# One product for the outputs and the state step of a delta-rule chunk, in a fused convolution and RWKV-7 block

## The chip, the cores and the metric

One core of a Trainium2 chip runs the whole block. The metric is device time in microseconds from launch to end, as the median of several executions. Engines are called PE (TensorE: matmuls, with their weight loads as PEld), DVE (VectorE), ACT (ScalarE), POOL (GpSimd) and SP (SyncE, which issues the DMAs).

## The reference, cut to what matters

The input x is 2048 tokens of 1024 channels, float32, one layer. An RMS norm with an adaptive scale and shift feeds one large input projection. Its parts go to a convolution branch (width 31, per channel) and to an RWKV-7 branch with 16 heads of 64 channels. Both are gated, projected, merged, projected once more and added to x, and a last RMS norm follows. The change lies in the RWKV-7 branch, whose core is a recurrence over tokens on a 64x64 state per head:

```
def step(state, inp):
    r_t, w_t, k_t, v_t, kk_t, b_t = inp
    sk = jnp.einsum('bhvk,bhk->bhv', state, kk_t)
    state = (state * w_t[:, :, None, :] - sk[..., None] * b_t[:, :, None, :]
             + v_t[..., None] * k_t[:, :, None, :])
    return state, jnp.einsum('bhvk,bhk->bhv', state, r_t)
...
o = _rwkv7_scan(r, decay.reshape(hd), k, v, kk, kk * a)
o = _layernorm(o, gn_g.reshape(RWKV_HEADS, RWKV_HEAD), gn_b.reshape(RWKV_HEADS, RWKV_HEAD), GN_EPS)
```

## The kernel before, in words

**Blocks, groups, pairs, chunks.** The 2048 tokens are four blocks of 512 (b). In a block the 1024 RWKV channels are four groups of 256 (g): 16 groups in all. A group is two pairs (q), a pair is two heads (hh) of 64 channels, which fill the 128 partitions. The 512 tokens of a block are eight chunks of 64 (c); chunks are counted in pairs, cc, with e = 0 for the even and 1 for the odd one.

**What fills PE.** For each block, every column tile of the input projection is a product of 24 matmuls (8 tiles of K, each three times, because the operands are split into a high and a low fp32r part) into one of two PSUM banks, ps_main. The order of the projections is written out by hand in FILL and LAST: k, r and v of a pair, then convolution values and gates. The output products of the end of the kernel (`wino`, tiles w_c) go into ps_main as well.

**How the rest is put between.** All other work is written as Python generators, called tasks. While the kernel is built, a planner keeps a modelled clock (`note`, lines 116 to 183, prices each instruction) and lets a task go on when the model says that what it waits for is there. After each matmul of a projection the planner is polled and may put a task's instructions next in the queues of the engines. So the order of every engine's instructions is fixed at build time; on the chip each engine takes its own queue in order and waits for semaphores. In the model an f32 product of PE costs `max(N_, 64) / 600 * 1.04` us if it uses all 128 rows and more than 64 columns of the array, with N_ the moving columns (line 137), about half of that or less if it uses 64 rows or 64 columns (`part`), and a change between the two kinds costs 0.13 or 0.27 us more (line 141).

**A pair** (`pair`, lines 980 to 1117) works on decays and keys and builds, per chunk, two operands in SBUF: KR (decayed kk and r side by side) and BK (scaled kk·a and k side by side). Lines 1071 to 1085 multiply BK by KR for all chunks and both heads, mask the 128x128 results and store them in As: for each pair, head and chunk a 128x128 matrix. Half of its columns belong to r (`rcol`), the other half to kk (`kcol`). These products wait with `joining` (line 298): while a chain runs they are held back by up to JOIN = 6 us unless the last product on PE was of the partial kind. Lines 1087 to 1094 transpose BK on PE into tk, with the two halves of tk's partitions for k and kk·a. At line 1101 the pair waits until the norm of the group two before is through, because uv has two buffers. Pairs run one after the other, and the evacuation of the next pair's k, r and v projections waits for a pair's end (line 1635). BK has one buffer.

**A group** (`group`, lines 1131 to 1362) sends the kk blocks of As through DRAM into a layout where POOL inverts 64 triangular 32x32 blocks at once (lines 1146 to 1175, tiles La, TT, itmp), gets them back into As, and in a locked stretch (lines 1211 to 1270, in which no other task may take a PSUM bank of the small pools) completes the inverses of the 64x64 triangles (Tn) and multiplies tk and the r columns of As by them (py, pg). From there on tk holds, per chunk, the k rows and the inverse-multiplied kk rows; As holds the matching r columns.

**The chain** (lines 1275 to 1314) is the loop over the eight chunks, in which the state S of the group's four heads is carried along. For each chunk c:

- PE: KR times S, two products (q) into columns 0 and 1 of the PSUM bank xo of that parity (`b_`); half of the partitions are the outputs' part from the old state, the other half what is needed for uv.
- ACT: Se = S times the chunk's decay pe, two instructions. DVE: adds the PSUM half to uv, 64x256.
- PE: state increment tk times uv, in an even chunk as two 128x128 products with 128 moving columns, in an odd chunk as four products of 64 columns by head.
- DVE: S = increment times pe plus Se, four instructions of 64x64.
- Only after an odd chunk: PE adds the r columns of As times uv for both chunks of the pair, eight products of 64 array columns and 64 moving columns, and ACT copies both output halves into O (which is uv's memory).

**The norm** (lines 1317 to 1362) normalizes O per head. For each of the two pairs in turn it waits until the gate projection exists (`G.gated`), loads two tiles zb and zr, transposes four 128x128 pieces of O into the bank late, scales on ACT, adds and multiplies on POOL and stores to z_d. `G.normed` is set at the second pair.

Of the kernel before, what the change touches and what calls it, by code (L numbers as in the profile page):

```python
# [82 lines left out]
def hybrid_block(ctx: ExitStack, tc: tile.TileContext, x, vecs, convk, w2a2, final_g, ada, w_in, w_co, w_ro, w_o, crow, out,  # L83
# [896 lines left out]
    def pair(G, q_, box):  # L980
# [105 lines left out]

        tk = l3.tile([P, NCH, P], F32, name="tk", tag="tk", bufs=TKB)
# [31 lines left out]
    def opened(b, g, h, lora):  # L1119
        G = Group()  # L1120
        G.b, G.g, G.h, G.lora, G.tri, G.pairs, G.chained, G.gated, G.normed = b, g, h, lora, 0, 0, False, False, False
        G.merged = False
# [8 lines left out]
    def group(G, before):  # L1131
# [18 lines left out]
        for half in range(2):  # L1150
            nc.sync.dma_start(La[64 * half:64 * half + 64], dAl)
        TT = lt.tile([P, 16, 32], F32, name="TT", tag="TT", bufs=1)
# [25 lines left out]
        for half in range(2):  # L1178
            nc.sync.dma_start(dTl[half], TT[64 * half:64 * half + 64])
        yield ok(dT)  # L1180
# [54 lines left out]

        def banks():
            return [p_.tile([P, NCH // 2, P], F32, name=n_, tag=n_) for p_, n_ in ((pl, "late"), (pa, "aux"))]
# [11 lines left out]
        with tc.high_priority(HP):  # L1249
# [23 lines left out]
        yield step(*tk)  # L1273
# [3 lines left out]
        for c in range(NCH):  # L1277
# [975 lines left out]
```

## Time and profile before

| | us |
|---|---|
| median of 3 runs | 2713.66 |
| lowest, highest | 2713.03, 2714.61 |
| the profiled execution, its own time | 2703.53 |
| its span, first to last instruction | 2701.8 |

The profile is one execution, and its durations belong to that one. Its time is 10.1 us below the median of the runs. Granted TensorE clock over the span: 0.989.

How to read it: nearly all instructions carry line 194, because a helper records every operation for the planner; so groups are told apart by their tiles, written out<-in with buffer numbers left out. "128*128" behind a PE instruction are the rows and columns of the array that it uses, the two sizes behind it are what moves through and how much, "x4" is how many instructions a row gathers. In a group's row, the numbers behind the bar are the busy time in us, the mean duration of one in ns, and the idle time of the engine just before them with what ended it.

| tiles | what it is |
|---|---|
| ps_main | projections and output products |
| aux<-KR,BK | the products of `pair` that become As |
| aux<-ident,BK | transposes into tk |
| xo<-S,KR | chain: old state |
| xo<-uv,tk | chain: state increment |
| xo<-uv,As, 128*64 | chain: outputs (64*64 is the locked stretch) |
| late<-ident,uv | transposes of the norm |

### The profile page before, as it was taken

The page shows a single profiled execution, that of the slowest core. Times are in us where ns is not written, and L with a number is a line of the kernel's source. Part 1 is how long each engine was busy: PE and PEld are TensorE (multiplying, and loading weights), DVE is VectorE, ACT ScalarE, POOL GpSimd, SP SyncE. Part 2 cuts the span into 40 slices and gives each one's busy share as a digit, 9 for nine tenths or more (in the row PEclk, how much of TensorE's full clock was granted, in tenths as well). Part 3 has the DMA queues.
Part 4 walks back from the last instruction along what each step waited for, and adds up shares of the span by engine and source line. Part 5 has one row for each costly group of instructions (what it writes and reads, how often), then busy time and mean ns, then how long its engine had stood idle before and what let it go on. Part 6 is the DMA issues. An engine that isn't in the chain of part 4 may idle for free.

```text
span 2701.8 us, 51029 instructions
## 1 busy us (share of the span) xinstructions
PE 2598.4 (96%) x18417; PEld 2092.2 (77%) x18417; DVE 2217.9 (82%) x3808; ACT 1188.2 (44%) x2343; POOL 1309.1 (48%) x1807
## 2 busy tenths in 40 slices
PE   6999999999999999999999999999999987899997
PEld 5778787887887887788888778788788766688886
DVE  7787889888879897888887878888988699888586
ACT  5544444453443433453434333434343454456443
POOL 1575748461738374626482857583716486000000
PEclk9999999999999999999999999999999998999999
DMA  9887778786877788868786888687756778789874
GB/s 346 277 297 268 270 255 282 264 277 221 275 237 266 224 290 268 267 202 274 231 281 214 293 282 262 236 285 231 241 170 219 251 251 285 252 319 333 313 265 164
DMA packets 396142, 705.04 MB, mean 261 GB/s; under 512 B 137065, under 2 KB 153777, under 8 KB 395889
## 3 DMA queue, kind: packets, MB, share of 16 engines
q1 hardware_dynamic: 395888, 701.78, 77.1%
q8 instruction: 145, 2.38, 0.4%
q14 instruction: 109, 0.88, 0.1%
HBM read 487.26 MB, written 213.26 MB: 259 GB/s over the span
## 4 chain that ended last, share of the span: by engine, by line
PE 51%; DVE 4%; DMA 2%; issue 1%; POOL 1%; ACT 0%; SPq 0%; DVEq 0%; ACTq 0%; POOLq 0%
PE ps_main L194 43%; PE aux L194 4%; PE xo L194 3%; PE late L194 2%; POOL w_c L194 1%; DVE S L194 0%; DVE cells L194 0%; DVE fc L194 0%; DVE h_lo L194 0%; DMA w_lo<-kl_in 0%; DMA hf<-xT 0%; DVE mr L194 0%; DVE As L194 0%; SPq L194 0%; DMA dn<-dN 0%
## 5 line engine op out<-in xcount | busy, mean ns | idle before, releaser
L194 PE MATMUL ps_main<-h_hi,w_hi 128*128 128x512 f32 x2304 | 925.8, 402 | 10.6 <-DVE lora L194 4.7
L194 PE MATMUL ps_main<-h_hi,w_lo 128*128 128x512 f32 x2304 | 922.0, 400 | 4.7 <-POOL w_lo L194 2.7
L194 PE MATMUL ps_main<-h_lo,w_hi 128*128 128x512 f32 x2304 | 923.3, 401 | 0.0
L194 DVE SCALAR_TENSOR_TENSOR acc<-u,ck,acc 128x512 f32<-128x512 f32 x928 | 698.2, 752 | 25.4 <-DVE acc L194 0.5
L194 PEld LDWEIGHTS ps_main<-h_hi,w_hi 128*128 128x128 f32 x2304 | 434.5, 189 | 108.5 <-issue 8.9
L194 PEld LDWEIGHTS ps_main<-h_hi,w_lo 128*128 128x128 f32 x2304 | 434.5, 189 | 101.5 <-POOL w_lo L194 4.9
L194 PEld LDWEIGHTS ps_main<-h_lo,w_hi 128*128 128x128 f32 x2304 | 434.6, 189 | 93.6 <-issue 5.7
L194 PE MATMUL ps_main<-h_hi,w_c 128*128 128x512 f32 x896 | 294.5, 406 | 19.3 <-DVE mr L194 9.4
L194 ACT ACTIVATE th<-ps_main 128x512 f32<-128x512 f32 x160 | 95.9, 599 | 348.6 <-PE ps_main L194 302.1
L194 POOL TENSOR_TENSOR TT<-TT,itmp 128x126 f32<-128x126 f32 (+22 forms) x496 | 211.8, 427 | 38.9
L194 POOL TENSOR_TENSOR itmp<-La,TT 128x126 f32<-128x126 f32 (+22 forms) x496 | 207.5, 418 | 41.5 <-issue 8.2
L194 PEld LDWEIGHTS ps_main<-h_hi,w_c 128*128 128x128 f32 x896 | 172.9, 193 | 63.5 <-issue 9.1
L194 POOL TENSOR_TENSOR w_lo<-w_st,w_hi 128x1024 fp32r<-128x1024 f32 x53 | 128.8, 2431 | 153.4 <-ACT w_hi L194 141.0
L194 PE MATMUL ps_main<-h_lo,w_c 128*128 128x512 f32 x448 | 182.1, 406 | 12.3 <-DVE h_lo L194 12.3
L194 ACT COPY uv<-xo 64x256 f32<-64x256 f32 (+1 forms) x192 | 81.1, 439 | 250.1 <-PE xo L194 188.5
L194 DVE SCALAR_TENSOR_TENSOR S<-xo,pe,Se 64x64 f32<-64x64 f32 x512 | 123.0, 280 | 51.0 <-PE xo L194 38.0
L194 PE MATMUL ps_main<-w_c,h_hi 128*128 128x512 f32 x448 | 140.0, 393 | 0.0
L194 ACT CAST w_c<-w_raw 128x512 fp32r<-128x512 f32 x168 | 102.8, 618 | 83.9 <-DMA w_raw<-wk_o 32.9
L194 DVE TENSOR_TENSOR As<-aux,maskA 128x512 f32<-128x512 f32 x128 | 82.4, 685 | 57.2 <-PE aux L194 56.6
L194 PEld LDWEIGHTS ps_main<-h_lo,w_c 128*128 128x128 f32 x448 | 86.5, 193 | 34.5 <-DVE h_lo L194 15.7
L194 ACT ACTIVATE t<-ps_main,mu 128x512 f32<-128x512 f32 x96 | 66.0, 687 | 107.2 <-PE ps_main L194 100.9
L194 ACT ACTIVATE Se<-S,pe 128x128 f32<-128x128 f32 x256 | 88.7, 395 | 43.5 <-DVE S L194 42.7
(294 smaller groups left out, 4559.2 us busy)
## 6 DMA issues: line engine op xcount, KB each, us to landing
w_hi<-kh_in SPq DMA_DIRECT2D x219, 512.0 KB
w_lo<-kl_in SPq DMA_DIRECT2D x219, 512.0 KB
w_st<-w_in_t SPq DMA_DIRECT2D x73, 512.0 KB
kh_in<-w_hi SPq DMA_DIRECT2D x71, 512.0 KB
kl_in<-w_lo SPq DMA_DIRECT2D x71, 512.0 KB
lny<-y_d SPq DMA_DIRECT2D x80, 256.0 KB
w_raw<-wk_o SPq DMA_DIRECT2D x56, 256.0 KB
ada_st<-ada_t SPq DMA_DIRECT2D x16, 512.0 KB
```

Source lines behind the costliest of these rows:

```text
L194: r = f(*a, **k)
```

## The change

As and tk are put side by side in one 128x128 matrix. After the locked stretch, its r columns are as before, and its kk columns, which are no longer needed, are overwritten with the values of tk: the k rows by four copies on ACT, the inverse-multiplied kk rows by the four copies on DVE that went to tk before. One product of As with uv then gives a chunk's outputs on one half of the partitions and the state increment on the other. It is done in each chunk, even or odd, in four products (pair and head) with all 128 columns of the array and 64 moving columns, added onto the outputs' part that KR times S left in the bank; the other half of the bank, whose value was added to uv, is set to zero by a memset first. The decay that the four DVE instructions multiplied in is now taken into BK before the transposes, by eight ACT instructions of 128x128 for each pair, after the products of BK and KR have read it. The state step becomes two DVE adds of 64x128. ACT copies the outputs after each chunk, 64x256 at a time, as many copies as before.

Two more edits: a group clears TT only when the group before has sent off its inverses (`inverted`); and the norm transposes and scales both pairs first, sets `normed`, and only then waits for the gate and loads zb and zr for each pair.

```diff
@@ pair, between the products for As and the transposes into tk
+        for c4 in range(NCH // 4):
+            yield used_up(BK)
+            for c in range(c4 * 4, c4 * 4 + 4):
+                bk = BK[:, c // 2, c % 2 * 128:c % 2 * 128 + 128]
+                nc.scalar.mul(bk, bk, pe[:, c:c + 1])
...
@@ group, before TT is cleared
+        yield when(lambda: before is None or before.inverted)
         TT = lt.tile([P, 16, 32], F32, name="TT", tag="TT", bufs=1)
...
@@ group, locked stretch
             for e in range(2):
                 for q in range(2):
-                    nc.vector.tensor_copy(tk[q][prow(e), e::2, :], py[q][prow(e)])
-        yield both(step(*tk), bank("late"))
+                    nc.scalar.copy(As[q][vrow(e), :, e::2, kcol(e)], by_head(tk[q][vrow(e), e::2, :]))
+            for e in range(2):
+                for q in range(2):
+                    nc.vector.tensor_copy(As[q][prow(e), :, e::2, kcol(e)], by_head(py[q][prow(e)]))
+        yield both(step(*As), bank("late"))
...
@@ group, chain
                 nc.vector.tensor_tensor(out=uv[pr_, c], in0=b_[pr_, 0:2], in1=uv[pr_, c], op=ALU.add)
-            yield step(uv)
-            if e == 0:
-                for q in range(2):
-                    nc.tensor.matmul(b_[:, 2 + q, :], R[q]["tk"][:, c, :], uv[:, c, q, :], start=False, stop=(q == 1),
-                                     skip_group_check=True)
-            else:
-                for q, hh, hs in every:
-                    nc.tensor.matmul(b_[hs, 2 + q, 0:64], R[q]["tk"][:, c, hs], uv[:, c, q, hs], start=False,
-                                     stop=(q + hh == 2), skip_group_check=True)
-            if e:
-                for n, (q, hh, hs) in enumerate(every):
-                    for i in range(2):
-                        nc.tensor.matmul(xo[i][vrow(i), q, hs], As[q][:, hh, c - 1 + i, rcol(i)], uv[:, c - 1 + i, q, hs],
-                                         start=False, stop=(n == 3), skip_group_check=True)
+                nc.vector.memset(b_[pr_, 0:2], 0.0)
+            yield step(uv, b_)
+            for n, (q, hh, hs) in enumerate(every):
+                nc.tensor.matmul(b_[:, q, hs], As[q][:, hh, c, :], uv[:, c, q, hs], start=False, stop=(n == 3),
+                                 skip_group_check=True)
             with tc.high_priority(HP):
-                for q, hh, hs in every:
-                    nc.vector.scalar_tensor_tensor(out=Sg[hs, q, hs], in0=b_[hs, 2 + q, slice(0, 64) if e else hs],
-                                                   scalar=R[q]["pe"][hs, c:c + 1], in1=Se[hs, q, hs],
-                                                   op0=ALU.mult, op1=ALU.add)
-            if e:
-                with tc.high_priority(HP):
-                    for i in range(2):
-                        nc.scalar.copy(O[vrow(i), cc], xo[i][vrow(i), 0:2])
+                for hs in (slice(0, 64), slice(64, 128)):
+                    nc.vector.tensor_tensor(out=Sg[hs, :, hs], in0=b_[pr_, 0:2, hs], in1=Se[hs, :, hs], op=ALU.add)
+                nc.scalar.copy(O[vrow(e), cc], b_[vrow(e), 0:2])
...
@@ group, norm
-        yield when(lambda: G.gated)
+        ocs = []
         for q in range(2):
...
+            ocs.append(oc)
+        G.normed = True
+        for q, oc in enumerate(ocs):
+            pr = 2 * g + q
+            yield both(when(lambda: G.gated), hx.room(2))
+            zb, zr = hx.take("zb"), hx.take("zr")
+            nc.sync.dma_start(zb, bv_dram[b][pr])
+            nc.sync.dma_start(zr, ro_dram[b][pr])
```

More of the change, by code (lines that the diff above doesn't have):

```diff
@@ L1121, in opened @@
         G.b, G.g, G.h, G.lora, G.tri, G.pairs, G.chained, G.gated, G.normed = b, g, h, lora, 0, 0, False, False, False
-        G.merged = False
+        G.merged = G.inverted = False
         G.prior, G.uv, G.As = Gs[-2] if len(Gs) > 1 else None, None, []
@@ L1179, in group @@
             nc.sync.dma_start(dTl[half], TT[64 * half:64 * half + 64])
+        G.inverted = True
         yield ok(dT)
@@ L1234, in group, with by_head @@
         yield both(step(Tn, uv), bank("xo", 2))
+        def by_head(t_):
+            return t_.rearrange("p c (h n) -> p h c n", h=2)
         def banks():
@@ L1272, in group @@
         Sg = S[g]
-        yield step(*tk)
+        yield step(*As)
         xo = [px.tile([P, 4, P], F32, name="xo", tag="xo") for _ in range(2)]
@@ L1342, in group @@
         yield ok(uv)
-        yield when(lambda: G.gated)
+        ocs = []
         for q in range(2):
             pr = 2 * g + q
-            yield hx.room(2)
-            zb, zr = hx.take("zb"), hx.take("zr")
-            nc.sync.dma_start(zb, bv_dram[b][pr])
-            nc.sync.dma_start(zr, ro_dram[b][pr])
             yield burst(free, bank("late"))
```

1 line of the change is left out of this document (removed).

## The prediction

> **What bounds the kernel now.** I read the busy table first, then the chain of waits, then the busy time by stages, then the groups of instructions by shape, and last the timeline around single products.
>
> ```profile
> PE 2598.4 (96%) x18417; PEld 2092.2 (77%) x18417; DVE 2217.9 (82%) x3808; ACT 1188.2 (44%) x2343; POOL 1309.1 (48%) x1807
> ...
> PE 51%; DVE 4%; DMA 2%; issue 1%; POOL 1%; ACT 0%; SPq 0%; DVEq 0%; ACTq 0%; POOLq 0%
> ```
>
> ```profile
> 50.00:2147.00 2097.00, 2063.19 (x15711) 1664.32 (x15710) 1734.84 (x2958) 891.92 (x1783) 1199.20 (x1724) 1.00 0.77 255
> 2147.00:2390.00 243.00, 208.16 (x1275) 161.10 (x1274) 214.16 (x337) 113.38 (x211) 108.54 (x74) 0.94 0.78 265
> ```
>
> The columns of the second fence are the stretch, its length, and the busy time of PE, weight loads, DVE, ACT and POOL. From 50 to 2147 us, where the sixteen groups run, PE is busy 2063 of 2097 us at full clock (the 1.00 behind POOL); only 34 us are idle. No other engine there is above 83% (DVE 1735 of 2097). So a microsecond added to PE's queue in this stage is a microsecond of time, and a microsecond saved elsewhere is worth at most a part of those 34. From 2147 to 2390 it is different: PE has 35 us of idle time, and DVE is 88% busy.
>
> What the chain's own products cost on PE is not their busy time, because matmuls overlap. It is what they push apart in the row of ps_main products.
>
> ```profile
> 253.17 0.39 PE L194 MATMUL ps_main<-h_hi,w_hi 128*128 128x512 f32 x1
> 253.40 0.39 PE L194 MATMUL ps_main<-h_lo,w_hi 128*128 128x512 f32 x1
> 253.63 0.60 PE L194 MATMUL xo<-S,KR 128*128 128x128 f32 x4
> ...
> 254.30 0.40 PE L194 MATMUL ps_main<-h_hi,w_hi 128*128 128x512 f32 x1
> ```
>
> ```profile
> 260.59 0.39 PE L194 MATMUL ps_main<-h_lo,w_hi 128*128 128x512 f32 x1
> 260.82 0.60 PE L194 MATMUL xo<-uv,tk 128*128 128x128 f32 x4
> ...
> 261.50 0.39 PE L194 MATMUL ps_main<-h_hi,w_hi 128*128 128x512 f32 x1
> ```
>
> ```profile
> 1338.11 0.40 PE L194 MATMUL ps_main<-h_lo,w_hi 128*128 128x512 f32 x1
> 1338.44 0.46 PE L194 MATMUL xo<-uv,tk 128*64 128x64 f32 x8
> 1338.72 0.64 PE L194 MATMUL xo<-uv,As 128*64 128x64 f32 x16
> ...
> 1339.63 0.40 PE L194 MATMUL ps_main<-h_hi,w_hi 128*128 128x512 f32 x1
> ```
>
> Undisturbed ps_main products stand 0.23 us apart (253.17 to 253.40). I measure from the last ps_main start ahead of a burst to the second one behind it, since the first behind it comes early and the second late, and take off two steps, 0.46. The KR·S burst then costs 254.30 − 253.40 − 0.46 = 0.44, the increment of an even chunk 261.50 − 260.59 − 0.46 = 0.45, and the increment of an odd chunk with the outputs of both chunks 1339.63 − 1338.11 − 0.46 = 1.06 us. Each f32 product is two instructions, so those bursts are 2, 2 and 4 + 8 products.
>
> **The change: PE.** There are 16 groups of 4 chunk pairs, 64 pairs. KR·S stays. Removed per pair: 0.45 + 1.06 = 1.51 us. Added per pair: two bursts of four products, weights 128x128 (As), only 64 columns moving, so 8 instructions each. The trace has no such shape. What sets its pace is the weight load.
>
> ```profile
> L194 PEld LDWEIGHTS xo<-S,KR 128*128 128x128 f32 x512 | 74.8, 190 | 17.0 <-issue 6.8 <-DVE S L194 0.6
> ...
> L194 PEld LDWEIGHTS xo<-uv,As 128*64 128x64 f32 x1024 | 35.8, 138 | 0.0
> ```
>
> ```profile
> 257.27 0.19 PEld L194 LDWEIGHTS ps_main<-h_lo,w_hi 128*128 128x128 f32 x1
> 257.37 0.19 PEld L194 LDWEIGHTS ps_main<-h_hi,w_lo 128*128 128x128 f32 x1
> ```
>
> A load of 64 columns lasts 138 ns and one of 128 columns 190: 0.8 ns per column on top of a fixed part. At 257.27 two full loads follow each other with no product between (behind a burst of another shape) and stand 0.10 us apart: that is the pace of loads alone. The KR·S burst, four loads and four products of 128 columns in 0.44 to 0.45, has a pace of 0.112. With 64 columns moving the product gets shorter but its load does not, so I price an instruction at 0.112 again: 8 × 0.112 = 0.90 us per chunk. Bounds: the pace of 64-column work from the odd burst, 8 instructions from 1338.44 to 1338.72, alternating between two column halves, so 0.07 each and 0.56 in all; and above, load and half-length product one after the other, 0.11 + 0.05, 1.28 in all. I take 0.90 because the nearest row, KR·S, has the same weights and shows the load fully overlapped. Per pair 1.80 − 1.51 = +0.29, times 64: **+18.4 us**. The bounds give −25 and +67.
>
> [...]
>
> **The change: lost company.** The odd burst works on 64-column halves of the array, KR·BK of the next pair on 64-row halves; call both tiled. The planner likes to put them side by side (line 303 holds KR·BK back by up to 6 us for it while a chain runs).
>
> ```profile
> 255.00 0.39 PE L194 MATMUL ps_main<-h_hi,w_hi 128*128 128x512 f32 x1
> ...
> 255.60 0.64 PE L194 MATMUL xo<-uv,As 128*64 128x64 f32 x16
> 256.18 1.16 PE L194 MATMUL aux<-KR,BK 64*128 64x128 f32 x16
> ...
> 257.61 0.40 PE L194 MATMUL ps_main<-h_hi,w_lo 128*128 128x512 f32 x1
> ```
>
> ```profile
> 136.50 0.39 PE L194 MATMUL ps_main<-h_hi,w_lo 128*128 128x512 f32 x1
> 136.82 1.16 PE L194 MATMUL aux<-KR,BK 64*128 64x128 f32 x16
> ...
> 138.26 0.40 PE L194 MATMUL ps_main<-h_lo,w_hi 128*128 128x512 f32 x1
> ```
>
> ```profile
> 2007.96 0.64 PE L194 MATMUL xo<-uv,As 128*64 128x64 f32 x16
> 2008.54 1.16 PE L194 MATMUL aux<-KR,BK 64*128 64x128 f32 x16
> ```
>
> Together they cost 257.61 − 255.00 − 0.46 = 2.15; alone 1.06 and 1.30: 0.21 saved each time. It happens 18 times in the timeline, first at 256.18, last at 2008.54. With no tiled burst left in the chain there is nothing to join: 18 × 0.21 = **+3.8 us** (0 if as many find another partner).
>
> **The change: DVE, ACT, POOL, SP.**
>
> ```profile
> L194 DVE SCALAR_TENSOR_TENSOR S<-xo,pe,Se 64x64 f32<-64x64 f32 x512 | 123.0, 280 | 51.0 <-PE xo L194 38.0 <-issue 4.7 <-ACT tk L194 2.4
> ...
> L194 DVE TENSOR_TENSOR uv<-xo,uv 64x256 f32<-64x256 f32 x128 | 53.9, 421 | 29.0 <-PE xo L194 25.2 <-ACT Se L194 1.0
> ...
> L194 DVE MEMSET S<- 128x256 f32 x4 | 1.1, 272 | 0.1
> ```
>
> ```profile
> L194 ACT ACTIVATE Se<-S,pe 128x128 f32<-128x128 f32 x256 | 88.7, 395 | 43.5 <-DVE S L194 42.7
> ...
> L194 ACT COPY uv<-xo 64x512 f32<-64x512 f32 x64 | 34.1, 582 | 100.7 <-PE xo L194 100.5
> ```
>
> DVE per chunk: four increments go, 123.0 / 128 = 0.96 us. A memset of 64x256 comes, between 0.27 (the SBUF memset as wide) and 0.42 (the add of that shape in PSUM), and two adds of 64x128, 0.29 each by interpolating 280 and 421. Net −0.11 to +0.04, times 128: −14 to +5 us on an engine that does not bound; worth nothing by itself. The copies of the inverse keep their count and size, into As instead of tk.
>
> ACT: 256 decay scalings of 128x128, priced by the Se row, 89 us; 64 copies of 64x512 (tk into As), 34 to 37 us. The output copies stay at 128 of 64x256. ACT in the group stage goes from 892 to about 1016 of 2097 us: free time hides it, 49% busy. Queued behind four scalings (1.4 us) are evacuations of ps_main; PE has two banks and a projection is 24 × 0.23 = 5.5 us, so that stays covered.
>
> The pair task gets a new wait: the scalings start only when both KR·BK bursts have read BK, and the transposes into tk wait for all eight, 2.8 us, part of it beside the mask products that free the aux banks anyway. I take +2 us per pair. Who waits: the next pair's k evacuation.
>
> ```profile
> 108.53 1.31 POOL L194 TENSOR_TENSOR vv<-rk,vv 128x512 f32<-128x512 f32 x1
> ```
>
> ```profile
> 110.63 0.74 DVE L194 SCALAR_TENSOR_TENSOR k<-ps_main,v,t 128x511 f32<-128x511 f32 x1
> ```
>
> ```profile
> 274.22 1.28 POOL L194 TENSOR_TENSOR vv<-rk,vv 128x512 f32<-128x512 f32 x1 [6.68 <-ACT Se L194]
> ```
>
> ```profile
> 298.07 0.72 DVE L194 SCALAR_TENSOR_TENSOR k<-ps_main,v,t 128x511 f32<-128x511 f32 x1
> ```
>
> The first pair ends at 109.84 and the next k follows at 110.63: no cover, so +2 once. The fourth ends at 275.50, 22.6 us ahead; such a cover hides it. Without it the cost would be 32 × 2 = 64 us. Sum of this: **+2** (0 to 4).
>
> In the locked stretch ACT copies tk into As behind the four uv copies, 4 × 0.58, so the chain starts about 2 us later; PE has projections meanwhile: nothing. The wait for the prior inversion before TT's memset is met long before in all groups but perhaps the last: nothing, 4 us at most. Norm: two transposes move ahead of two loads each on SP; uv is released earlier, and the group results are needed only after 2147: −1, between −6 and +6, since the stage from 2147 is bound by DVE and moving work between POOL and DVE there can go either way.
>
> **Idle time of the chain.**
>
> ```profile
> L194 PE MATMUL xo<-S,KR 128*128 128x128 f32 x512 | 79.7, 278 | 4.7 <-DVE S L194 4.5
> ...
> L194 PE MATMUL xo<-uv,tk 128*128 128x128 f32 x256 | 42.1, 289 | 10.2 <-DVE uv L194 9.1
> ```
>
> PE lost 14.9 us here to a late DVE. The planner (line 137) prices the new product by its 64 columns, 4 × 0.11 = 0.44, where I expect 0.90, so PE will arrive later than planned and find DVE ready more often. I give back a third, **−5 us** (−15 if all goes, +10 if the new order brings as much as it has brought here).
>
> **Sum**: 18.4 + 3.8 + 2 − 1 − 5 = +18.2 us. The profiled execution took 2703.53 us (span 2701.8 and 1.7 around it), 10.1 below the median of the runs, 2713.66. So 2721.7 in such an execution, and 2713.66 + 18.2 = **2731.9** as a median. By the bounds of the smaller terms (0 to 3.8, 0 to 4, −6 to +6, −15 to +10) this forecast's own range is 2718 to 2748.
>
> **Rivals.** *The product is paced by its 64 moving columns.* For it: the 0.07 of 64-column work, and one array shape for the whole chain. Against: loads in a row 0.10 apart with no product between. Price: 8 × 0.07 = 0.56, so 1.12 − 1.51 = −0.39 per pair, −25, and with the other terms −25.2: 2688. It decides if the new burst stands below 0.75. Chance 0.08. [...]
>
> *No change.* The product costs what I say, but nearly all idle time of the chain goes (−15) and the last stage gains (−6): 18.4 + 3.8 + 2 − 15 − 6 = +3.2: 2717. For it: the idle time is there. Against: much of it is a few single long waits that any order can have. Chance 0.12.
>
> *Pairs become late.* ACT, fuller, takes 10 us more per pair in place of 2 and covers of 10 to 20 us begin to fail in about one pair of three, 2 us each: +22 more: 2754. Against: the cover of 22.6. Chance 0.06.
>
> *Load and short product don't overlap:* 1.28 per chunk, +67 in place of 18.4: 2780. Against: the KR·S burst. Chance 0.04.
>
> **Numbers.** Forecast 0.70, rivals 0.08, 0.12, 0.06, 0.04. 0.2% is 5.4 us, about what a measurement of this kernel can tell from no change. Slower by more: 0.70 + 0.06 + 0.04 = 0.80; within: 0.12; faster: 0.08. The range 2712 to 2748 holds the forecast and the no-change case and leaves out 0.18.
>
> **What the profile after would show.** Right: bursts xo<-uv,As 128*128 128x64 x8 that cost 0.90 by the same measure, loads 0.11 apart; no KR·BK behind a tiled burst, all 64 at 1.30; the group stage longer by 15 to 25 us with PE still at 98%; ACT near 1314 us; DVE nearly as before; a longer wait at 110 us. Wrong: bursts of 0.6 or less; or PE's idle time in the group stage moved by more than 15 us; or many pairs whose next k evacuation waits for them.

## The result and the profile after

The kernel after takes **2758.4 us** at the median (2753.8 to 2761.7), the kernel before 2714.1 beside it: a ratio of **1.0169, 95% interval 1.0153 to 1.0184**, 44 us slower. The sign was forecast, the size was not: 2731.9 was the number, 2748 the upper end. The profiled execution after took 2759.96 us, 56.4 more than that of before, which lay some 10 us below its own median. The accounts below are made of these two executions, so they have to explain 56, not 44; the 12 between are taken for idle and slow time of single executions, since a kernel's instructions are the same each time; that was not shown. Three single executions of kernels further down took 4297, 5836 and 9328 us; they are left out of medians and ratios.

The busy table after, and the shares of the chain of waits:

```profile
PE 2633.2 (95%) x17649; PEld 2142.8 (78%) x17649; DVE 2177.4 (79%) x3684; ACT 1290.7 (47%) x2663; POOL 1293.7 (47%) x1803
...
PE 80%; DVE 7%; DMA 5%; issue 3%; ACT 2%; POOL 2%; SPq 2%; DVEq 0%; ACTq 0%; POOLq 0%
```

The same by stages, cut where before was cut, 3 us behind the start of the last stage (2143.8 us before, 2193.0 after):

```profile
50.00:2196.00 2146.00, 2094.42 (x15001) 1708.93 (x15000) 1703.85 (x2839) 993.14 (x2095) 1190.16 (x1725) 0.99 0.75 250
2196.00:2439.00 243.00, 206.41 (x1198) 163.39 (x1197) 196.41 (x320) 110.81 (x213) 102.34 (x69) 0.93 0.75 250
```

The group stage is longer by 49 us (2097 to 2146), and that is nearly the whole loss. PE is busy 31 us more in it (2063.2 to 2094.4) and idle 18 us more (33.8 to 51.6); and the granted clock, 1.00 before, is 0.99, so some of the 31 is not work either.

A chunk's new burst in the timeline, with nothing beside it:

```profile
262.71 0.39 PE L194 MATMUL ps_main<-h_lo,w_hi 128*128 128x512 f32 x1
262.94 0.39 PE L194 MATMUL ps_main<-h_hi,w_lo 128*128 128x512 f32 x1
263.17 1.00 PE L194 MATMUL xo<-uv,As 128*128 128x64 f32 x8
263.98 0.48 PE L194 MATMUL ps_main<-h_hi,w_hi 128*128 128x512 f32 x1
264.29 0.40 PE L194 MATMUL ps_main<-h_lo,w_hi 128*128 128x512 f32 x1
```

By the measure of the prediction it costs 264.29 − 262.94 − 0.46 = 0.89 us; the median over all bursts of eight between two ps_main products is 0.895. The price was 0.90. The groups that answer to those of before, busy time and mean of one, then the idle time ahead of them and what ended it:

```profile
L194 PE MATMUL ps_main<-h_hi,w_hi 128*128 128x512 f32 x2304 | 926.8, 402 | 27.1 <-DVE k L194 11.9 <-DVE lora L194 4.7 <-issue 2.3
...
L194 PE MATMUL xo<-uv,As 128*128 128x64 f32 x1024 | 131.6, 272 | 10.0 <-DVE xo L194 9.3
...
L194 ACT ACTIVATE BK<-BK,pe 128x128 f32<-128x128 f32 x256 | 80.7, 391 | 21.2 <-PE aux L194 21.1
...
L194 DVE TENSOR_TENSOR S<-xo,Se 64x128 f32<-64x128 f32 x256 | 73.6, 288 | 56.7 <-PE xo L194 45.0 <-issue 6.8 <-ACT ta L194 1.6
...
L194 ACT COPY As<-tk 64x512 f32<-64x512 f32 x64 | 36.4, 618 | 0.2
...
L194 DVE MEMSET xo<- 64x256 f32 x128 | 34.8, 272 | 15.9
```

The first row is the news. In the kernel before it reads as follows; the wait for k, 1.0 us there, is not among its three longest:

```profile
L194 PE MATMUL ps_main<-h_hi,w_hi 128*128 128x512 f32 x2304 | 925.8, 402 | 10.6 <-DVE lora L194 4.7 <-DVE r L194 1.8 <-DVE vv L194 1.2
```

**An account that closes.** From the starts of all products in a trace I took, for each stretch between two ps_main products, the pace of what lies between: 0.2295 us for a ps_main product, 0.112 for a 128-column one, the measured pace of the smaller shapes (KR·BK alone, sixteen instructions, costs 1.30), 0.215 for each entry into tiled work (joined, KR·BK and the odd burst cost 2.15, alone 1.30 and 1.06). What a stretch takes beyond that is idle time or slow clock. Before: work other than ps_main 460.7 us, idle and slow 63.6 in the group stage and 56.3 in the last. After: 482.0, 94.5 and 60.1. So +21.3 of work, +30.9 and +3.8 of idle and slow time: 56.0 of 56.4. (By the medians the last two come to some 23, an estimate: 44 less the work.) Work was forecast at +22.2. The miss is idle time in the group stage.

**Where it is.** The first pair, in the timeline of the kernel after:

```profile
110.18 1.29 POOL L194 TENSOR_TENSOR vv<-rk,vv 128x512 f32<-128x512 f32 x1 [2.88 <-ACT rk L194]
...
110.86 0.40 PE L194 MATMUL ps_main<-h_hi,w_lo 128*128 128x512 f32 x1
...
111.20 1.04 ACT L194 CAST w_hi<-w_st 128x1024 fp32r<-128x1024 f32 x1
...
112.27 0.69 ACT L194 ACTIVATE t<-ps_main,mu 128x512 f32<-128x512 f32 x1
...
113.59 0.75 DVE L194 SCALAR_TENSOR_TENSOR k<-ps_main,v,t 128x511 f32<-128x511 f32 x1 [0.43 <-ACT carry L194]
...
114.39 0.79 PE L194 MATMUL ps_main<-h_hi,w_hi 128*128 128x512 f32 x1 [3.14 <-DVE k L194]
...
114.99 0.63 PE L194 MATMUL ps_main<-h_lo,w_hi 128*128 128x512 f32 x1
...
119.68 0.63 PE L194 MATMUL aux<-lw,wlo 128*128 128x512 f32 x1
...
120.70 0.39 PE L194 MATMUL ps_main<-h_hi,w_lo 128*128 128x512 f32 x1
120.93 0.40 PE L194 MATMUL ps_main<-h_hi,w_hi 128*128 128x512 f32 x1
```

In the kernel before, ACT's first step for k ran ahead of the pair's end:

```profile
107.13 0.69 ACT L194 ACTIVATE t<-ps_main,mu 128x512 f32<-128x512 f32 x1
```

The pair's last product on GpSimd ends at 111.47 (before: 109.84), and k follows 2.1 us later, where it was 0.8. So k is 3.0 us late, and only 1.6 of it is the pair: the rest is ACT's queue, where t now stands behind the pair's last copies and a cast of weights of 1.04 us. PE waits 3.14 us. Then comes what the forecast had no term for: from 114.39 to past 119.68 products take 0.63 us and come 0.43 apart instead of 0.39 and 0.23, so PE ran at half clock for 6 us and lost some 2.7 more. The granted clock, the third number from the right, says the same, 0.50; below it the kernel with JOIN 0.0, whose first pair makes PE wait 3.15 us:

```profile
110.30:113.60 3.30, 0.96 (x5) 1.00 0.47 179
113.70:120.40 6.70, 6.00 (x14) 0.50 0.90 294
120.60:124.00 3.40, 3.40 (x17) 1.00 0.00 0
```

```profile
114.30:117.50 3.20, 3.20 (x9) 0.50 0.98 293
117.80:121.00 3.20, 3.20 (x15) 1.00 0.37 138
```

So with the same wait came half clock for 6.8 us in one kernel and for 3.4 in another. All such stretches in the traces, but for the one that a trace ends in, last 3.4 us or a multiple of it (3.41, 6.83 and 10.24 in the kernels before and after). In the kernel after the 432nd ps_main product starts 5.7 us later than before; the term for this pair was 2. Half clock also came with a wait of 1.91 us, at 1905.8 in the kernel with the scaling alone, and with one of 2.40 us, at 2222.7 in the kernel after (0.50 from 2223.0 to 2229.8), while one of 2.43 us, at 1882.9 in the kernel after, was not followed by it: the length of a wait alone doesn't tell.

The worst one stands near the end of the groups:

```profile
2091.66 11.83 DVE L194 SCALAR_TENSOR_TENSOR acc<-u,ck,acc 128x512 f32<-128x512 f32 x15
...
2098.54 1.27 POOL L194 TENSOR_TENSOR vv<-rk,vv 128x512 f32<-128x512 f32 x1
...
2103.40 0.74 DVE L194 SCALAR_TENSOR_TENSOR k<-ps_main,v,t 128x511 f32<-128x511 f32 x1
2104.06 0.74 DVE L194 SCALAR_TENSOR_TENSOR r<-ps_main,v,t 128x511 f32<-128x511 f32 x1
...
2104.19 0.79 PE L194 MATMUL ps_main<-h_hi,w_hi 128*128 128x512 f32 x1 [5.98 <-DVE k L194]
2104.78 0.63 PE L194 MATMUL ps_main<-h_lo,w_hi 128*128 128x512 f32 x1
2105.21 0.63 PE L194 MATMUL ps_main<-h_hi,w_lo 128*128 128x512 f32 x1
```

The pair is late (its last product ends at 2099.81), k comes 3.6 us after that, behind the last of the fifteen convolution taps on VectorE, and PE waits 5.98 us and goes on at half clock. ACT had done its part for k by 2100.48, so VectorE's queue makes most of the delay behind the pair. In all PE waits for k 5 times, 11.9 us, where before had 1.0; and undisturbed ps_main products at half clock cost 11.6 us in the group stage against 3.1. That is 19 of the 31. Of the other 12, some 7 are a balance of many waits for others, up or down by a few us each, and the rest isn't resolved. Where idle time lies is not yet what caused it; that is for the experiments.

### The profile page after: what moved, and what is told of

Same layout as the page of the kernel before. It is cut to its first block, busy times and chain, and to the rows that moved or that the text cites. A ratio compares the mean times of both kernels' runs of the same rounds, so it can differ in the third digit from the quotient of the medians.

```text
span 2758.2 us, 49724 instructions
## 1 busy us (share of the span) xinstructions
PE 2633.2 (95%) x17649; PEld 2142.8 (78%) x17649; DVE 2177.4 (79%) x3684; ACT 1290.7 (47%) x2663; POOL 1293.7 (47%) x1803
## 4 chain that ended last, share of the span: by engine, by line
PE 80%; DVE 7%; DMA 5%; issue 3%; ACT 2%; POOL 2%; SPq 2%; DVEq 0%; ACTq 0%; POOLq 0%
PE ps_main L194 64%; PE aux L194 6%; PE xo L194 6%; PE late L194 3%; SPq L194 2%; DMA w_lo<-kl_in 1%; DVE acc L194 1%; PE ps_f L194 1%; DVE h_lo L194 1%; DMA w_st<-w_in_t 1%; DMA hf<-xT 0%; DVE mr L194 0%; DVE w_lo L194 0%; DMA lny<-y_d 0%; DVE As L194 0%
## 5 line engine op out<-in xcount | busy, mean ns | idle before, releaser
L194 PE MATMUL ps_main<-h_hi,w_hi 128*128 128x512 f32 x2304 | 926.8, 402 | 27.1 <-DVE k L194 11.9
L194 POOL TENSOR_TENSOR itmp<-La,TT 128x126 f32<-128x126 f32 (+22 forms) x496 | 206.9, 417 | 41.9 <-issue 11.9
L194 POOL TENSOR_TENSOR TT<-TT,itmp 128x126 f32<-128x126 f32 (+22 forms) x496 | 204.4, 412 | 38.9
L194 PEld LDWEIGHTS xo<-uv,As 128*128 128x128 f32 (+1 forms) x2048 | 164.2, 165 | 30.9 <-DVE xo L194 15.3
L194 PE MATMUL xo<-uv,As 128*128 128x64 f32 (+1 forms) x2048 | 166.5, 247 | 13.0 <-DVE xo L194 9.3
L194 ACT CAST w_c<-w_raw 128x512 fp32r<-128x512 f32 x168 | 102.5, 618 | 73.6 <-DMA w_raw<-wk_o 32.8
L194 DVE TENSOR_TENSOR S<-xo,Se 64x128 f32<-64x128 f32 x256 | 73.6, 288 | 56.7 <-PE xo L194 45.0
```

Of the source, the lines that this page charges most:

```text
L194: r = f(*a, **k)
```

## The experiments

Ratios are to the kernel before, measured on the same chip, with 95% intervals; before took 2711 us at the median in all of them. Differences between kernels are of their medians. The first theory was that late pairs lose the time (scalings and the hold of line 303), with rivals in the planner's price, VectorE's zeroing, and the edits of order.

**Decay back in the state step** (after, BK unscaled):

```
-                nc.scalar.mul(bk, bk, pe[:, c:c + 1])
...
-                    nc.vector.tensor_tensor(out=Sg[hs, :, hs], in0=b_[pr_, 0:2, hs], in1=Se[hs, :, hs], op=ALU.add)
+                    nc.vector.scalar_tensor_tensor(out=Sg[hs, q, hs], in0=b_[pr_, q, hs], scalar=R[q]["pe"][hs, c:c + 1],
+                                                   in1=Se[hs, q, hs], op0=ALU.mult, op1=ALU.add)
```

> The change with one part undone: BK is not scaled, and the decay is multiplied in at the state step again, by four DVE instructions of 64x64 in place of two adds. The chain's new product stays. Late pairs (my theory): the longer pairs and the halved clock after the stalls they make are most of the 26 us that the prediction missed, so this gives back 12 to 22 us of the 44: 2736 to 2746 us, with the waits of ps_main for k (12.7 us in the changed kernel's group stage) below 3. Rival, mispriced product: the order of the queues is wrong because the planner takes 0.44 for 0.90 us, which stays: 2752 to 2762. Rival, the memset in the chain: stays too, and DVE gets 0.4 us more per chunk: 2758 to 2770.

Measured: 2775.2 us, 1.0234 (1.0214 to 1.0253), 17 slower than after. A miss for the theory: PE's waits for k did go (1.0 us), yet the idle and slow time of the group stage was 101.8. The 512 scaled adds came back for 256 plain ones, 123.1 us busy on VectorE for 73.6; that these 50 us are the reason is not shown.

**Only the scaling** (before, with BK scaled and plain adds of 64x64):

> The kernel before with one part of the change alone: BK is scaled by the decay on ACT before the transposes, and the state step adds without multiplying, still in four instructions; the chain's products, the norm and the rest are as before. Late pairs: PE work is unchanged, but pairs end 3 to 5 us later, which stalls the first and the last pairs and drops the clock: 8 to 20 us over before, 2722 to 2734. Both rivals: no change, 2711 to 2717.

Measured: 2712.8 us, 1.0007 (0.9997 to 1.0017): no change in the time, as both rivals said, again a miss for the theory. Yet PE waits for k 3 times, 7.9 us, where before had 1.0: the lateness is there. The adds, 0.218 us against 0.280, free 31 us of VectorE; that this is what pays for it is argued, not shown.

**No hold** (after, JOIN 6.0 to 0.0):

> The changed kernel, with the constant JOIN set from 6 to 0, so that KR and BK products are no longer held back for a tiled partner that the new chain never offers. Late pairs: pairs that meet a chain end up to 12 us earlier, so 5 to 15 us are given back: 2743 to 2753. Mispriced product and memset: no change, 2754 to 2762.

Measured: 2737.3 us, 1.0093 (1.0076 to 1.0109): 21 us, half of the loss, come back, more than any of the theories said. Its ps_main row:

```profile
L194 PE MATMUL ps_main<-h_hi,w_hi 128*128 128x512 f32 x2304 | 928.2, 403 | 20.9 <-DVE k L194 7.5 <-DVE vv L194 5.8 <-DVE lora L194 4.7
```

Idle and slow time of the group stage is 68.8, near the 63.6 of before, at the same work (482.0). So in this kernel holding KR·BK back for a burst that no longer exists costs 21 us. What is left, 26 us over before, is little more than the 21.3 of work.

**The planner's price put right** (after; line 137 prices a full-width product by at least 128 columns):

```
-                c = max(N_, 64) / 600 * (0.27 if M_ <= 64 and K_ <= 64 else 0.53 if part else 1.04)
+                c = max(N_, 64 if part else 128) / 600 * (0.27 if M_ <= 64 and K_ <= 64 else 0.53 if part else 1.04)
```

> The changed kernel, with the planner's price of a full-width product raised to that of 128 columns if fewer move, so 0.22 us for each product of the chain in place of 0.11; nothing else. Mispriced product: idle time of PE in the group stage falls by 12 to 25 us: 2733 to 2746. Late pairs: the pairs stay as long, the planner only knows better when PE comes: 2750 to 2760.

Measured: 2757.2 us, 1.0163 (1.0147 to 1.018), no different from after, as the theory of late pairs said. The wrong price is not the cause.

**No hold, in the kernel before** (JOIN 0.0):

> The kernel before with JOIN 6.0 set to 0.0, so that a chunk's KR.BK pair never waits for a partial-row burst to join. Theory (the hold pays where it has a partner: joined, the pair spares the array its change of mode, and only in the kernel after, where no partial-row burst is left, is it a bare delay): 2715 to 2726 us, 4 to 15 slower, with the KR,BK burst at about 1.5 us alone, as after. Rival (a held pair is a late pair in either kernel, partner or not, and what JOIN 0.0 gave after, 21 us, comes here too): 2690 to 2705 us. Rival (the hold matters only once the pairs have lost their slack to the chain's longer bursts): 2709 to 2715 us.

Measured: 2705.4 us, 0.9984 (0.9971 to 0.9997). Outside all three: slightly faster, 6 us, though half the joined bursts are gone (9 in the trace for 18). The hold is no gain there, and far from 21 us of loss.

**An idle product in each chunk's burst** (before):

```
+    zero = cst.tile([P, 8], F32, name="zero")
...
+            nc.tensor.matmul(b_[:, 2, 64:72], R[0]["tk"][:, c, :], zero, start=False, stop=False, skip_group_check=True)
```

> The kernel before with one idle product more in each chunk's burst: the 128x128 tile of tk again, against 8 columns of zeros, 128 times in all, priced as low by the planner as the new product is after; nothing else moves. By the load pace of the trace (0.224 us for one 128-column f32 product) that is 28.7 us of TensorE work. Theory (TensorE work in the chain's bursts costs the kernel its own time, once, and the rest of what after lost comes from elsewhere): 2736 to 2746 us. Rival (work put into the chain's bursts draws waits and half-clock stretches after it, so that each microsecond costs about two, as 21 of work went with 31 of idle and slow clock after): 2755 to 2775. Rival (idle time of the chain absorbs it): 2711 to 2725.

Measured: 2758.1 us, 1.0176 (1.016 to 1.0193), 47 more, which looked like the rival. It was spoilt: the 32 bytes of zeros at the start of the constants moved every later tile, see the shift below. With JOIN 0.0 beside it:

> The kernel before with JOIN 0.0 and the same idle product in each chunk's burst (28.7 us of TensorE work). Theory (the hold is what made 47 us out of 28.7): 2705 and 28.7, so 2728 to 2739 us. Rival (work in the chain's bursts costs more than itself with or without the hold): 2745 to 2757.

Measured: 2747.9 us, 1.0136 (1.0114 to 1.0158), spoilt in the same way.

**Three products of four** (after; the second head of the second pair is left out):

> The kernel after with the fourth product of each chunk's burst left out (the second head of the second pair: its state increment and its output are then not computed); every other operation is as after. TensorE has 128 x 0.224 = 28.7 us less work, 7 less than before has. Theory (work costs its own time once, the hold and the later pairs the rest): 2725 to 2735 us. Rival (idle and slow clock follow the work): 2700 to 2716. Rival (the loss is held up by VectorE's queue and the late pairs, not by TensorE's work): 2745 to 2758.

Measured: 2752.9 us, 1.0151 (1.0134 to 1.0167), as the last of the three said. The work fell to 453.1 us as meant, and idle and slow time rose to 115.0:

```profile
L194 PE MATMUL ps_main<-h_hi,w_hi 128*128 128x512 f32 x2304 | 929.4, 403 | 37.1 <-DVE k L194 23.7 <-DVE lora L194 4.7 <-DVE vv L194 2.3
```

A shorter burst gained 5 us for 29 of work. PE waited 23.7 us for k, 12 more than after, which is over half of the 20.5 that idle and slow time rose by. That late pairs are the limit here is argued, not shown.

**The edits of order alone** (before, with the wait for the inverse and the norm's two pairs first):

> The kernel before with only the two edits of order: the next group's matrices wait until the group before has its inverted ones, and the norm turns both pairs before it takes up the gate. Every theory that puts the loss into the product, the hold and the pairs says no change: 2707 to 2717 us. Rival (the norm's edits, which let the next group's banks and the gate's buffers go at other times, are where the 31 us of idle come from): 2725 to 2745.

Measured: 2720.5 us, 1.0035 (1.0023 to 1.0048): 9 us slower, between the two. Its idle time lies in the last stage (74.5 against 56.3), where the trace has one wait of 16.35 us, at 2293.5, for the norm's work on GpSimd. To see the same edits in the new kernel I undid them there, with and without the hold.

**The product without the edits of order**, JOIN 0.0 and JOIN 6.0:

> The kernel after with JOIN 6.0 set to 0.0 and the norm's edits and the inverted wait undone: of the change only the product, its zeroing and the decay in tk are left. Theory (three causes that add: 21 us of TensorE work, the hold, the norm's edits): the kernel before with JOIN 0.0 took 2705 us, and 21 of work makes 2727: 2720 to 2732 us. Rival (the work draws waits after it, as the dose on the kernel before did, 47 us for 28.7): 2737 to 2750. Rival (the norm's edits cost nothing here): 2735 to 2740, as with JOIN 0.0 alone.

> The kernel after with only the norm's edits and the inverted wait undone, JOIN 6.0 left. Theory (the three causes add): 9 us less than after, 2744 to 2753 us. Rival (with the hold the pairs are late whatever the norm does): 2755 to 2761. Rival (late pairs and the norm's order feed each other): under 2740.

Measured: 2747.2 us (1.014, 1.012 to 1.0159) and 2774.3 us (1.0237, 1.0215 to 1.0259). Both theories of adding causes fail: here the edits gain 10 to 16 us instead of costing 9. The first run lies in the range of the rival by which work draws waits, the second outside all three. The hold costs 27. The profiled execution with the hold took 2786.5 us, 12 above its median, so its rows are high. Its ps_main row:

```profile
L194 PE MATMUL ps_main<-h_hi,w_hi 128*128 128x512 f32 x2304 | 931.1, 404 | 34.0 <-DVE k L194 16.6 <-ACT h_hi L194 7.1 <-DVE lora L194 4.7
```

and without it:

```profile
L194 PE MATMUL ps_main<-h_hi,w_hi 128*128 128x512 f32 x2304 | 926.9, 402 | 16.3 <-DVE k L194 7.9 <-DVE lora L194 4.7 <-DVE th L194 1.6
```

**Three products of four, JOIN 0.0, old order:**

> As the product with JOIN 0.0 and the old norm, but with the fourth product of each chunk's burst left out (the second head of the second pair is then not computed), 28.7 us less TensorE work. Theory (work counts once): 28.7 less than the whole product there, so 2693 to 2705 us. Rival (the end is set by the last pairs and the last group's inverse on GpSimd, and not by TensorE's work): within 8 us of the whole product, 2715 to 2732.

Measured: 2707.4 us, 0.9995 (0.9984 to 1.0007): 40 less than with four, for 28.7 us of work, which lies between the two ranges. Without the hold, TensorE's work counts, and by the account some 10 us of idle and slow time in the group stage went with it. Against the three of four with hold and new order it is 46 us less.

**The shift alone** (before, with the 8 columns of zeros and nothing that uses them):

> The kernel before with nothing but 32 bytes more per partition at the start of the constants, so that every later tile lies 32 bytes further on; no instruction uses them. In both runs with the idle product, whose zeros lay there, the 128x512 products came 234 ns apart at the median instead of 230, and there are 8928 of them. Theory (the shift of the addresses is what slowed them, and so some 30 of the dose's 47 us): 2736 to 2746 us, with a median step of 233 to 235 ns. Rival (the idle product slowed them): 2707 to 2717 us at 230 ns.

Measured: 2727.8 us, 1.0065 (1.0045 to 1.0086): 17 slower, between the two ranges, though the products do step at 234 ns at the median, as in the two other kernels with the shift; all seventeen without it have 230 or 231. Thirty-three undisturbed steps of the kernel before, first and last:

```profile
1014.11 0.39 PE L194 MATMUL ps_main<-h_hi,w_lo 128*128 128x512 f32 x1
...
1021.66 0.39 PE L194 MATMUL ps_main<-h_hi,w_lo 128*128 128x512 f32 x1
```

and forty-one with the shift:

```profile
1009.68 0.39 PE L194 MATMUL ps_main<-h_hi,w_lo 128*128 128x512 f32 x1
...
1019.25 0.40 PE L194 MATMUL ps_main<-h_lo,w_hi 128*128 128x512 f32 x1
```

7.55 / 33 = 0.2288 us against 9.57 / 41 = 0.2334, with the same products in the same order. The steps of before vary by place: the mean of the some 7800 undisturbed ones went from 229.9 to 233.3 ns, 27 us in sum, where the kernel lost 17. Where the rest came back isn't shown.

**The idle product without the shift** (its zeros in 512 bytes behind the weights and activations):

> The kernel before with the idle product in each chunk's burst again, its zeros now in a tile of 512 bytes behind the weights and activations, so that no operand of the 128x512 products is moved by less than that. In the first dose the even burst grew by 0.227 us and the odd one by 0.118, so the dose is 22 us of TensorE work. Theory (work in the chain's bursts costs its own time, once): 2729 to 2738 us, the products 230 ns apart. Rival (work draws idle time after it): 2745 to 2760.

Measured: 2740.7 us, 1.0117 (1.0099 to 1.0134), 30 more (27 to 36), between theory and rival. An even chunk's burst:

```profile
260.50 0.39 PE L194 MATMUL ps_main<-h_hi,w_hi 128*128 128x512 f32 x1
260.73 0.39 PE L194 MATMUL ps_main<-h_lo,w_hi 128*128 128x512 f32 x1
260.96 0.33 PE L194 MATMUL xo<-zero,tk 128*128 128x64 f32 x2
261.13 0.66 PE L194 MATMUL xo<-uv,tk 128*128 128x128 f32 x4
261.55 0.48 PE L194 MATMUL ps_main<-h_hi,w_lo 128*128 128x512 f32 x1
261.87 0.40 PE L194 MATMUL ps_main<-h_hi,w_hi 128*128 128x512 f32 x1
```

It costs 261.87 − 260.73 − 0.46 = 0.68, at the median 0.227 more than before; the odd burst grew by 0.166. That makes 64 × 0.227 + 64 × 0.166 = 25 us of work (28 by the account) for 27 to 36 us of time: work in the chain's bursts costs itself, or a little more, and its idle and slow time in the group stage is near that of before (64.9).

**A blind hold** (before, line 303 without `and not kind[0]`, so that a partner no longer ends the wait):

> The kernel before with the hold made blind: while a chain is open, a KR.BK pair always waits its 6 us, and a partial-row burst no longer ends the wait. No work is added or taken. Theory (the hold without a partner is what makes the idle and half-clock time of after: 26 us there, 57 with the old norm): 2731 to 2765 us, and the idle and slow time of the group stage 25 to 55 us above that of before. Rival (the hold costs only beside the longer bursts of the new product): 2707 to 2720.

Measured: 2704.8 us, 0.9975 (0.9965 to 0.9985): the theory fails, the kernel gains 6 us, though only 1 joined burst is left of 18. With JOIN 0.0 (2705.4) it is the fastest that computes all, ahead of both given ones. A hold that never waits and one that always does gain the same here, so a difference of 6 us between two planned orders says little about the part that was changed.

**The blind hold with the idle product, and with the scaling:**

> The kernel before with the blind hold and the idle product of the clean dose together. Alone the blind hold took 6 us off (2705) and the dose put 30 on (2741). Theory (the hold costs where the chain's bursts are longer on TensorE): 20 to 50 us over the sum of the two, 2755 to 2785 us. Rival (the two only add; the length of the bursts is not what makes the hold dear): 2729 to 2742.

> The kernel before with the blind hold and the scaling of BK by the decay together (the state step as plain adds). Alone the scaling changed nothing (1.0007) and the blind hold took 6 us off. Theory (a held pair that then waits for its scaling comes too late for the next pair's k, and this is what the hold costs after): 2720 to 2740 us. Rival (the two only add): 2702 to 2712.

Measured: 2725.3 us (1.0045, 1.0027 to 1.0064) and 2709.2 us (0.9997, 0.9987 to 1.0007). The first is below even the sum, the second is the sum: neither longer bursts nor scalings alone make the hold dear. The three together were not run. But the scaling again brings waits for k, 8.8 us, where the blind hold alone has 1.4.

**Decay in the state step, JOIN 0.0:**

> The kernel after with the decay back in the state step (four scaled adds on VectorE, BK unscaled) as in the first experiment, and JOIN 0.0. With JOIN 6.0 that kernel took 2778 us. Theory (product and hold together cost 20 us or more, with or without the scaling): 2748 to 2760 us. Rival (the hold needs the scaling behind it): 2768 to 2782.

Measured: 2801.1 us, 1.0333 (1.0314 to 1.0353), outside both: without the scaling behind it, taking the hold away makes the new product's kernel 26 us slower.

The accounts together, in us (the shifted kernels left out); "k" is PE's time waiting for k. Work, idle time and k are those of the one profiled execution, whose own time stands beside the median and lies up to 12 us off it:

| kernel | median | profiled | work | group stage, idle and slow | last stage | k |
|---|---|---|---|---|---|---|
| before | 2714.1 | 2703.5 | 460.7 | 63.6 | 56.3 | 1.0 |
| its edits of order | 2720.5 | 2717.8 | 460.9 | 59.1 | 74.5 | 2.9 |
| JOIN 0 | 2705.4 | 2704.1 | 462.0 | 67.8 | 50.7 | 1.0 |
| idle product | 2740.7 | 2739.8 | 488.6 | 64.9 | 63.3 | 1.5 |
| blind hold | 2704.8 | 2697.8 | 464.3 | 54.9 | 55.3 | 1.4 |
| blind hold, idle product | 2725.3 | 2716.6 | 491.8 | 47.1 | 54.1 | 1.0 |
| scaling | 2712.8 | 2720.0 | 460.0 | 75.2 | 61.3 | 7.9 |
| scaling, blind hold | 2709.2 | 2710.4 | 464.1 | 69.6 | 53.2 | 8.8 |
| after | 2758.4 | 2760.0 | 482.0 | 94.5 | 60.1 | 11.9 |
| after, price | 2757.2 | 2751.8 | 482.0 | 89.5 | 57.1 | 7.5 |
| after, JOIN 0 | 2737.3 | 2733.6 | 482.0 | 68.8 | 59.1 | 7.5 |
| product, old order | 2774.3 | 2786.5 | 482.0 | 122.0 | 59.8 | 16.6 |
| product, old order, JOIN 0 | 2747.2 | 2747.0 | 482.0 | 65.4 | 76.0 | 7.9 |
| after, three of four | 2752.9 | 2754.1 | 453.1 | 115.0 | 62.4 | 23.7 |
| three of four, old order, JOIN 0 | 2707.4 | 2710.1 | 453.3 | 55.9 | 77.6 | 5.3 |
| after, decay in the step | 2775.2 | 2772.5 | 481.8 | 101.8 | 64.9 | 1.0 |
| the same, JOIN 0 | 2801.1 | 2802.5 | 481.3 | 121.4 | 75.7 | 1.0 |

## Why the prediction was wrong in size

**The step that failed.** The forecast put the loss at 18.2 us; it is 44. The largest piece that an experiment isolates is the hold of line 303, in the step "lost company": the sum took it at +3.8, for the joins that are lost, and at nothing as a delay of pairs that have no partner. Without the hold the kernel after takes 21 us less and is 26 over before: inside the forecast's range, which ends 34 over it. Next come the terms for the pair task and for idle time, below. How the hold's delay turns into time was not followed pair by pair.

The stated range is also narrower than its terms: the bounds of the small terms, each at its end, reach from 2711 to 2756, not from 2718 to 2748. 2758 lies outside both.

**Right: the product.** It is paced by its weight loads: they stand 0.111 us apart at the median, as its instructions do with 64 moving columns and those of KR·S with 128. The burst costs 0.895 us where 0.90 was put, against bounds of 0.56 and 1.28. No burst is left to join, and KR·BK alone costs 1.30 as before. Work rose by 21.3 where 18.4 + 3.8 = 22.2 was forecast, and the clean idle product shows that such work is paid once, or little more. Both rivals on the pace of the product are out. What was right here is the mechanism; it covers half of the loss.

**Right in kind: the side engines.** ACT 1290.7 for some 1314; zeroing took 0.272 us, the cheap end of its bounds, and an add 0.288 for 0.29. The order's edits came to +4 in the last stage, for −1 within −6 to +6; but the runs with them alone, +9 in the kernel before and −10 to −16 in the new one, show that this was no constant.

**Wrong: the pair task, "+2".** The sentence that fails is "The fourth ends at 275.50, 22.6 us ahead; such a cover hides it." One pair's cover was taken for the cover of all. The scaling makes PE wait for k, and this is shown by seventeen kernels: the eight without the scaling have 1.0 to 2.9 us, the nine with it 5.3 to 23.7, the first pair's 3.1 or 3.2 among them each time. After has 11.9. What these waits cost in the end is less clear: the planned order of ACT and VectorE makes part of the two longest, and three kernels without the hold keep 5.3 to 7.9 us of them with idle and slow time near that of before. The rival with late pairs came near the time (2754), but thought of 2 us in one pair of three, and took the scalings alone to do it; here there are five waits, two of them over 3 us, and the scaling in the kernel before moves the time by nothing. That the number agrees is no evidence.

**Wrong: no price for the clock.** With the first pair's wait of 3.1 us came 6.8 us of half clock in three kernels and 3.4 in the other six that have it. By the granted clock, the group stage of after ran 41 us at half clock, that of before 14. The ps_main products in it cost 8.5 us more than before, and nothing in the sum stood for it.

**Wrong: idle time given back, "−5".** For the two rows from which it was worked out it came true: 4.7 + 10.2 = 14.9 us ahead of KR·S and the increment became 0.7 + 10.0 = 10.7. But idle and slow time as a whole grew by 35 all the same. A share of one row's idle time is no forecast of an order's.

**Wrong: no price for the hold.** The prediction saw that nothing is left to join, and counted only the lost joins. In the kernel after, and in the same one with the old order, the hold costs 21 and 27 us. Why there and not in the kernel before stays open: by the runs it is neither the longer burst nor the scaling alone, and with neither hold nor scaling the new product's kernel was slowest of all (2801).

**Open.** Over the kernels of the table the group stage has 47 to 75 us of idle and slow time with the old product (mean of eight 62.8) and 56 to 122 with the new one (mean of nine 92.7). The nine are of three kinds. Three have the scaling and no hold: 55.9, 65.4 and 68.8, no more than the old product. So neither the new burst nor the zeroing ahead of it, which all three have, makes the idle time by itself. Four have the scaling and the hold: 89.5 to 122.0. Two have the decay in the step: 101.8 with the hold and 121.4 without, and hardly a wait for k. In after and its like, then, the idle time comes with the hold. In the kernel before, a hold without a partner, the longer burst and the scaling were tried alone, and the hold with each of the others, and none of these made it; all three at once were not run, and that is the nearest account left. Why the two with the decay in the step are slow is not known.

## What to carry to other kernels

The eight instructions of the new burst, with 128 weight columns and 64 moving ones, whose loads follow each other, took 0.895 us, 0.112 each, the pace of 128 moving columns; priced by the weight columns, that part of a forecast can be exact, as it was here. In an order that is planned ahead, look up the slack of every task that is made longer, the first and the last among them, because a few uncovered waits can cost more than their length: here 6.8 us at half clock came with a wait of 3.14 us, and 3.4 with one of 1.91. When a change removes the partner of a heuristic that waits for one, take the wait away with it and measure it in both kernels: doing so changed the time by −6, −21, −27 and +26 us in four kernels of this study.

## What the hardware showed

Moving every later tile by 32 bytes per partition slowed 128x512 products from 0.2288 to 0.2334 us in undisturbed rows, and the kernel by 17 us with not one instruction more in its loop. Which operand's address matters wasn't tried. And a wait of 3.14 us was followed by 6 us of work at half clock, one of 5.98 likewise, and, in the kernel with the scaling alone, one of 1.91 us by 3.4. The first cost some 2.7 us beyond its own length. One of 2.43 us in the kernel after was not followed by half clock. Stretches at half clock lasted 3.4 us or a multiple, and the same wait of 3.1 us was followed by 3.4 in some kernels and 6.8 in others.
